# A two-layer streaming encoder trunk: full-height matmuls in attention, and another opening

## The chip, the cores and the metric

One core of a Trainium2 chip runs the whole program. The metric is the device time of one execution in microseconds (us); the kernel before is given by the median of three runs. The engines are named PE (matmul), PEld (loading of a matmul's stationary operand, which can overlap PE), DVE (vector), ACT (scalar), POOL (GpSimd) and SP (the queue from which nearly all transfers are issued).

## The reference, cut to what matters

544 tokens (512 of a prompt, 32 of a running stream, "the sample") go through two layers. What the change touches is the attention of each layer:

```python
q = einsum('blr,rc->blc', rmsnorm(cq, q_norm_l), w_uq_l)      # 8 heads, 128 + 64 wide
q_nope, q_pe = q[..., :128], rope(q[..., 128:], pos)
lat_new, kpe_new = rmsnorm(ckv, kv_norm_l), rope(kr, pos)     # 256 wide; 64 wide, shared by the heads
# prompt: 512 queries on 512 keys, chunks of 64 masked; sample: 32 queries on 128 cached + 32 new keys
s = (einsum('bqhd,bkhd->bhqk', q_nope, k_nope) + einsum('bqhr,bkr->bhqk', q_pe, k_pe)) * scale
o = einsum('bhqk,bkhd->bqhd', softmax(s), v)
```

Ahead of the first layer's combined input projection stands an RMSNorm, whose sum of squares over 1024 features is the other thing touched:

```python
h = x * rsqrt(mean(x * x, axis=-1) + EPS) * norm_mix_l
cq, ckv, kr, hq, hf, hi, hg, ga, gb = split(h @ w_in_l, ...)
```

## The kernel before, in words

Features lie on the 128 partitions and tokens along them. Each float32 operand of a large product is split into a high part (rounded to the matmul's format, a copy on ACT) and a low part (the rest, a subtraction on DVE, or on POOL for attention's weights), and a product is three matmuls: high by high, high by low, low by high. `linear` (L198) runs such products over 8 row blocks and two halves of 272 tokens; `load_w` fetches a weight tile and splits it (L175 on ACT, L176 on DVE or POOL). Weight tiles of one kind share three raw buffers and four buffers each for high and low parts.

**The opening.** The input comes in eight blocks x_0 to x_7, by SP, with a vector of small constants (`vec`) and the first weight tile (`raw_first`) between x_0 and x_1. For every block `prep` makes hhi (ACT, L263) and hlo (DVE, L264). Squares of the blocks (ACT L279 for the even ones, POOL or DVE L281 for the odd ones) are added on POOL and DVE (L283, L284), a matmul with ones (`pn_m`, L234) sums over partitions, and a square root and a reciprocal give the norm's factor r. Products hf, hq and hi of layer 0 run ahead of r; hg needs a PSUM bank that is freed only when hf has been multiplied by r.

**Attention.** Heads are taken one after another. `attend` is a generator whose ten steps are laid between the products of other work (merge gates, the second branch's projection, queries and keys of the next head). `block(qb)` makes the scores of 128 queries (L736 to L738), masks them, and calls `softmax` (DVE maximum, ACT exponential with sum, DVE reciprocal and multiplication, L719 to L723). The rotary part has the queries in one tile `q4` of four 32-row bands (high, high, low, low) and the keys in `krh` (128 rows: the 64 rows twice) and `krl` (64 rows):

```python
nc.tensor.matmul(ps, q4[:, qs], krh[:, ks], start=False, stop=False)
nc.tensor.matmul(ps, q4[0:64, qs], krl[:, ks], start=False, stop=True)
```

`turn` transposes the probabilities on PE (L764) and splits them, `weigh` multiplies them with the values (L778). The sample's 32 queries are the last rows of the last 128: `sample_scores` makes their scores for 160 keys with the same five matmuls, copies 32 rows out of PSUM and runs the softmax on them; `sample_turn` transposes 128 and 32 keys apart (L799, L800) and splits twice; `sample_weigh` (L812) runs three matmuls over 128 rows and three over 32. One score is thus five matmuls, of which the fifth has 64 rows; there are 4 blocks and one sample score for each of 8 heads and 2 layers, 80 in all.

The order on each engine is fixed when the kernel is built: a list scheduler places every instruction by its own estimate of when it can run, starting from the order of the code; on the chip each engine then takes its list strictly in order.

Of the kernel before, what the change touches and what calls it, by code (L numbers as in the profile page):

```python
# [9 lines left out]
F32 = mybir.dt.float32  # L10
F32R = mybir.dt.float32r
U8 = mybir.dt.uint8
AF = mybir.ActivationFunctionType
# [38 lines left out]
class Late:  # L52
    """A value whose instructions come with its first use, or within the product before."""
# [10 lines left out]
class Pieces:  # L64
    """Weights of n row blocks, of which each group of eight is fetched at its first use."""
# [13 lines left out]
class Side:  # L79
    """Work whose instructions are laid between those of the large products."""  # L80
# [8 lines left out]
    def pace(self, rate):  # L89
        """Steps to take for each tick of the large products."""  # L90
        self.rate, self.owed = rate, 0.0
# [23 lines left out]
def trunk(ctx, tc, io):  # L115
# [17 lines left out]
    one = tmp.tile([P, P], F32, tag="t", name="one")  # L133
    nc.vector.memset(one, 1.0)
    ones = const.tile([P, P], F32R, name="ones")
    nc.scalar.copy(ones, one)
    eps = const.tile([P, 1], F32, name="eps")
    nc.vector.memset(eps, EPS)

# [99 lines left out]
    class Norm:  # L239
        """Sum of squares over feature blocks, as they come."""  # L240
# [16 lines left out]
    def prep(x, gcol, norm, name, vector=False):  # L257
        """Split of gain * x, and its share of the norm's sum."""
# [7 lines left out]

    norm = Norm("in")
    h = []
    xs = [bt(f"x_{j}", F32) for j in range(ND)]
    nc.sync.dma_start(xs[0], io["x"][:, 0, :])  # L270
    nc.sync.dma_start(vec, io["vec"])
    first = fetch_w(io["w_in"][0, U_HF], ND * P, "first")
    for j in range(1, ND):
        nc.sync.dma_start(xs[j], io["x"][:, j, :])
    for j in range(ND):
        h.append(prep(xs[j], V_MIX + j, None, f"in{j}"))
    for j in range(ND):
        if j % 2 == 0:
            nc.scalar.activation(xs[j], xs[j], AF.Square)  # L279
        else:  # L280
            (nc.gpsimd if j < 4 else nc.vector).tensor_mul(xs[j], xs[j], xs[j])  # L281
    for j in range(2, ND):
        (nc.gpsimd if j < 6 else nc.vector).tensor_add(xs[j % 2], xs[j % 2], xs[j])  # L283
# [12 lines left out]
    # Lower bounds of the forget gates: softmax over the layers, cumulated.  # L296
# [34 lines left out]
    for l in range(L):  # L331
# [21 lines left out]
        if l == 0:  # L353
            # The first products run while the norm is still on its way.
            early[U_HF] = product(U_HF, "hf0_", first)
# [9 lines left out]
        with ExitStack() as mixer:  # L365
# [4 lines left out]
            krl = mp.tile([64, KW], F32R, name=f"krl{l}")  # L370
# [729 lines left out]
```

## Time and profile before

| | |
|---|---|
| median of three runs (lowest, highest) | 1913.16 us (1912.61, 1913.16) |
| span of the profiled execution | 1910.8 us |
| PE busy, PEld busy | 1887.2 us (99%), 1847.6 us (97%) |
| DVE, ACT, POOL busy | 1092.7 us (57%), 797.1 us (42%), 312.2 us (16%) |
| chain that ended last | PE 97%, DVE 1%, DMA 1% |
| mean granted TensorE clock | 0.997 |

Times are counted from the span's start. In rows of the timeline the columns are start, duration, engine, line, operation, written tile <- read tiles, size (rows*columns of the stationary operand where it is a matmul) and, in brackets, how long the engine had been idle and what ended that. Matmuls are pipelined, so their printed durations overlap: what one costs on PE is the distance from its start to the next one's. In rows of busy times by stretch stand the stretch, its length, the busy time of PE, PEld, DVE, ACT and POOL with the number of instructions, the granted TensorE clock as a share of full speed, the busy share of the DMA engines and their GB/s.

### The profile page before, as it was taken

To read this page: it belongs to the slowest core of one execution; us is meant where nothing else is said; L and a number is where in the kernel's file an instruction comes from. 1 tells how busy PE (TensorE), PEld (TensorE's weight loads), DVE (VectorE), ACT (ScalarE), POOL (GpSimd) and SP (SyncE) were. 2 spreads that over 40 slices of the span, in tenths; PEclk is the share of its full clock that TensorE was granted. 3 is DMA by queue.
4 is the path that set the end of the run, shared out by engine and by line. 5 is a ranking of instruction groups with operands and counts; after the bars stand their busy time and mean duration, and the time that the engine had idled before them with its cause. 6 is when DMAs were issued, how large, how long until landed. Compare 5 with 4: busy or idle time off the path is not lost.

```text
span 1910.8 us, 36056 instructions
## 1 busy us (share of the span) xinstructions
PE 1887.2 (99%) x14680; PEld 1847.6 (97%) x14680; DVE 1092.7 (57%) x2113; ACT 797.1 (42%) x1454; POOL 312.2 (16%) x474
## 2 busy tenths in 40 slices
PE   7999999999999999999999999999999999999997
PEld 7999999899999999999999999998999999999997
DVE  7765865666465555533375667656655655555224
ACT  4222866554344333332232248564533433333231
POOL 3011021221212222100011110212112122222001
PEclk9999999999999999999999999999999999999999
DMA  5121432333542222234322124323235422222332
GB/s 181 57 70 67 131 122 83 95 102 104 194 158 89 89 89 89 89 95 125 102 91 70 57 80 143 119 80 107 93 126 190 138 85 87 87 88 87 103 96 75
DMA packets 75526, 197.29 MB, mean 103 GB/s; under 512 B 10208, under 2 KB 14304, under 8 KB 75360
## 3 DMA queue, kind: packets, MB, share of 16 engines
q1 hardware_dynamic: 75360, 194.98, 30.9%
q8 instruction: 116, 1.90, 0.4%
q14 instruction: 50, 0.41, 0.1%
HBM read 165.68 MB, written 24.81 MB: 100 GB/s over the span
## 4 chain that ended last, share of the span: by engine, by line
PE 97%; DVE 1%; DMA 1%; issue 0%; SPq 0%; ACT 0%; DVEq 0%; ACTq 0%
PE ps_uv L198 14%; PE ps_ua L198 14%; PE ps_d L198 13%; PE ps_gate L198 10%; PE ps_pa L198 5%; PE ps_o L198 5%; PE A L401 3%; PE ps_q L198 3%; PE ps_pb L198 3%; PE ps_hg L198 3%; PE ps_hq L198 2%; PE ps_hi L198 2%; PE ps_hf L198 2%; PE ps_cq L198 2%; PE sc L736 2%; PE ps_v L710 2%
## 5 line engine op out<-in xcount | busy, mean ns | idle before, releaser
L176 DVE TENSOR_TENSOR wlo_d<-raw_d,whi_d 128x512 fp32r<-128x512 f32 x96 | 62.5, 655 | 149.5 <-ACT whi_d L175 149.5
L198 PE MATMUL ps_uv<-hlo_f,whi_uv 128*128 128x272 f32 x704 | 145.9, 289 | 0.0
L198 PE MATMUL ps_ua<-hlo_f,whi_ua 128*128 128x272 f32 x704 | 145.9, 289 | 0.0
L198 PE MATMUL ps_ua<-hhi_f,wlo_ua 128*128 128x272 f32 x704 | 145.8, 288 | 0.0
L198 PE MATMUL ps_ua<-hhi_f,whi_ua 128*128 128x272 f32 x704 | 145.6, 288 | 0.0
L198 PE MATMUL ps_uv<-hhi_f,whi_uv 128*128 128x272 f32 x704 | 145.6, 288 | 0.0
L198 PE MATMUL ps_uv<-hhi_f,wlo_uv 128*128 128x272 f32 x704 | 145.4, 288 | 0.0
L198 PE MATMUL ps_d<-il,whi_d 128*128 128x272 f32 x660 | 136.9, 289 | 0.0
L198 PE MATMUL ps_d<-ih,wlo_d 128*128 128x272 f32 x660 | 136.6, 288 | 0.0
L198 PE MATMUL ps_d<-ih,whi_d 128*128 128x272 f32 x660 | 136.2, 288 | 0.0
L175 ACT CAST whi_d<-raw_d 128x512 fp32r<-128x512 f32 x96 | 55.8, 585 | 175.5 <-PE ps_d L198 143.7
L175 ACT CAST whi_ua<-raw_ua 128x512 fp32r<-128x512 f32 x88 | 54.7, 621 | 165.3 <-PE ps_ua L198 157.9
L175 ACT CAST whi_uv<-raw_uv 128x512 fp32r<-128x512 f32 x96 | 59.6, 621 | 142.5 <-PE ps_uv L198 134.1
L198 PEld LDWEIGHTS ps_ua<-hhi_f,wlo_ua 128*128 128x128 f32 x704 | 110.8, 188 | 0.2
L198 PEld LDWEIGHTS ps_ua<-hhi_f,whi_ua 128*128 128x128 f32 x704 | 110.9, 188 | 0.0
L198 PEld LDWEIGHTS ps_uv<-hhi_f,whi_uv 128*128 128x128 f32 x704 | 110.9, 188 | 0.0
L198 PEld LDWEIGHTS ps_uv<-hhi_f,wlo_uv 128*128 128x128 f32 x704 | 110.7, 188 | 0.0
L198 PEld LDWEIGHTS ps_ua<-hlo_f,whi_ua 128*128 128x128 f32 x704 | 110.4, 188 | 0.0
L198 PEld LDWEIGHTS ps_uv<-hlo_f,whi_uv 128*128 128x128 f32 x704 | 110.4, 188 | 0.0
L198 PEld LDWEIGHTS ps_d<-ih,whi_d 128*128 128x128 f32 x660 | 103.6, 188 | 0.0
L198 PEld LDWEIGHTS ps_d<-il,whi_d 128*128 128x128 f32 x660 | 103.6, 188 | 0.0
L198 PEld LDWEIGHTS ps_d<-ih,wlo_d 128*128 128x128 f32 x660 | 103.2, 188 | 0.0
(469 smaller groups left out, 5274.8 us busy)
## 6 DMA issues: line engine op xcount, KB each, us to landing
raw_ua<-in_w_up SPq DMA_DIRECT2D x44, 512.0 KB, 3.2
raw_uv<-in_w_up SPq DMA_DIRECT2D x44, 512.0 KB, 3.2
raw_gate<-in_w_in SPq DMA_DIRECT2D x32, 512.0 KB, 3.7
raw_d<-in_w_dn SPq DMA_DIRECT2D x32, 512.0 KB, 3.5
gates<-z_gate SPq DMA_DIRECT2D x32, 272.0 KB, 2.9
raw_pa<-in_w_pa SPq DMA_DIRECT2D x16, 512.0 KB, 3.5
raw_wo<-in_w_o SPq DMA_DIRECT2D x16, 512.0 KB, 3.7
raw_d<-in_w_dn SPq DMA_DIRECT2D x16, 384.0 KB, 3.1
```

The source lines that it names most:

```text
L175: nc.scalar.copy(hi[:, :n], part)
L176: (nc.gpsimd if pool else nc.vector).tensor_sub(lo[:, :n], part, hi[:, :n])
L198: nc.tensor.matmul(ps[t][:, 0:n], w, x[:, t * n:(t + 1) * n], start=(i == 0), stop=(i == last),)
L401: nc.tensor.matmul(ps[:, s], kk[:, s], qq[:, s], start=True, stop=True)
L710: nc.tensor.matmul(ps[:, :2 * P], lat[k][x][:, s], wv[k][w], start=(i == 0), stop=(i == 5))
L736: nc.tensor.matmul(ps, a[:, qs], b[:, ks], start=(i == 0), stop=False)
```

## The change

In attention: `krl` gets 128 rows (the low part of both copies of the rotary keys), and the fifth matmul of a score reads all of `q4`. The sample's softmax runs on all 128 rows straight from PSUM, into a buffer of the probabilities' own pool of four (a 96-column strip of it is zeroed on POOL); its two transposes are 128 by 128, its split is one copy and one subtraction, and all six of its weighing matmuls read 128 rows. In the opening: `raw_first` comes in two halves, both issued from ACT's queue; its splits stand right behind the first block's hhi and hlo in the code; all squares are on ACT, all additions on DVE, none on POOL. Docstrings and comments are dropped too, so line numbers differ by a few.

```diff
+    first = wts.tile([P, 1024], F32, tag="raw", name="raw_first", bufs=3)
     nc.sync.dma_start(xs[0], io["x"][:, 0, :])
+    nc.scalar.dma_start(first[:, 0:512], io["w_in"][0, U_HF][:, 0:512])
     nc.sync.dma_start(vec, io["vec"])
-    first = fetch_w(io["w_in"][0, U_HF], ND * P, "first")
+    nc.scalar.dma_start(first[:, 512:1024], io["w_in"][0, U_HF][:, 512:1024])
...
     for j in range(ND):
         h.append(prep(xs[j], V_MIX + j, None, f"in{j}"))
+        if j == 0:
+            first_ws = load_w(None, ND, P, "hf0_0", raw=first)
     for j in range(ND):
-        if j % 2 == 0:
-            nc.scalar.activation(xs[j], xs[j], AF.Square)
-        else:
-            (nc.gpsimd if j < 4 else nc.vector).tensor_mul(xs[j], xs[j], xs[j])
-    for j in range(2, ND):
-        (nc.gpsimd if j < 6 else nc.vector).tensor_add(xs[j % 2], xs[j % 2], xs[j])
+        nc.scalar.activation(xs[j], xs[j], AF.Square)
+        if j > 1:
+            nc.vector.tensor_add(xs[j % 2], xs[j % 2], xs[j])
...
-            krl = mp.tile([64, KW], F32R, name=f"krl{l}")
+            krl = mp.tile([P, KW], F32R, name=f"krl{l}")
...
-                    nc.vector.tensor_sub(krl, kr[0:64, :], krh[0:64, :])
+                    nc.vector.tensor_sub(krl, kr, krh)
...
-                        nc.tensor.matmul(ps, q4[0:64, qs], krl[:, ks], start=False, stop=True)
+                        nc.tensor.matmul(ps, q4[:, qs], krl[:, ks], start=False, stop=True)
...
-                        sP = ap.tile([SS, NK], F32, tag="sP", name=f"sP{nm}")
-                        nc.scalar.copy(sP, ps[P - SS:P, :NK])
-                        softmax(sP, sP, SS, f"{nm}_s")
+                        sP = ap.tile([P, 512], F32, tag="p", name=f"sP{nm}", bufs=4)
+                        nc.gpsimd.memset(sP[:, NK:2 * P], 0.0)
+                        softmax(sP[:, :NK], ps[:, :NK], P, f"{nm}_s")
...
-                        nc.tensor.transpose(ps[:, 0:SS], sP[:, 0:PAST], ident[0:SS, 0:SS])
-                        nc.tensor.transpose(ps[0:SS, SS:2 * SS], sP[:, PAST:NK], ident[0:SS, 0:SS])
+                        for a in range(2):
+                            nc.tensor.transpose(pw[:, a, :], sP[:, a * P:(a + 1) * P], ident)
...
-                        split(sph[:, 0:SS], spl[:, 0:SS], ps[:, 0:SS])
-                        split(sph[0:SS, SS:2 * SS], spl[0:SS, SS:2 * SS], ps[0:SS, SS:2 * SS])
+                        split(sph, spl, pw[:, :, P - SS:P])
...
-                        for a, rr in ((0, P), (1, SS)):
+                        for a in range(2):
...
-                                    ps[:, 0:SS], v[0:rr, 4 + a, vo:vo + P], p[0:rr, a * SS:(a + 1) * SS],
+                                    ps[:, 0:SS], v[:, 4 + a, vo:vo + P], p[:, a, :],
```

Where instructions move, first ACT in the opening, before (`x` tiles are the input blocks; L279 is a square, L263 an hhi, L175 the split of a weight tile's half):

```order
L263 ACTIVATE hhi_in_116<-x_91,vec 128x544
L279 ACTIVATE x_89<-x_89 128x544
L263 ACTIVATE hhi_in_120<-x_92,vec 128x544
L279 ACTIVATE x_91<-x_91 128x544
L263 ACTIVATE hhi_in_124<-x_93,vec 128x544
L175 CAST whi_hq_0_0_237<-raw_hq_0_235 128x512
L263 ACTIVATE hhi_in_128<-x_94,vec 128x544
L279 ACTIVATE x_93<-x_93 128x544
L263 ACTIVATE hhi_in_132<-x_95,vec 128x544
L175 CAST whi_hq_0_4_241<-raw_hq_0_235 128x512
```

And the same engine after the change, from the fifth hhi on (L256 is an hhi, L284 a square, L168 a split):

```order
L256 ACTIVATE hhi_in_133<-x_87,vec 128x544
L284 ACTIVATE x_85<-x_85 128x544
L256 ACTIVATE hhi_in_137<-x_88,vec 128x544
L284 ACTIVATE x_86<-x_86 128x544
L256 ACTIVATE hhi_in_141<-x_89,vec 128x544
L284 ACTIVATE x_87<-x_87 128x544
L256 ACTIVATE hhi_in_145<-x_90,vec 128x544
L284 ACTIVATE x_88<-x_88 128x544
L284 ACTIVATE x_89<-x_89 128x544
L168 CAST whi_hq_0_0_238<-raw_hq_0_236 128x512
L284 ACTIVATE x_90<-x_90 128x544
L168 CAST whi_hq_0_4_242<-raw_hq_0_236 128x512
```

The split of the second product's weights (whi_hq) has moved from between the hhi's to behind all of them and behind seven of the eight squares.

PE at the end of product hf and the beginning of product hq, before:

```order
L198 MATMUL ps_hf_0_186<-hhi_in_128,wlo_hf_0_4_183 128x272 x2
L198 MATMUL ps_hq_0_245<-hhi_in_108,whi_hq_0_0_237 128x272
L198 MATMUL ps_hf_0_186<-hlo_in_129,whi_hf_0_4_182 128x272 x2
L198 MATMUL ps_hq_0_245<-hhi_in_108,whi_hq_0_0_237 128x272
L198 MATMUL ps_hf_0_186<-hhi_in_132,whi_hf_0_4_182 128x272 x2
L198 MATMUL ps_hf_0_186<-hhi_in_132,wlo_hf_0_4_183 128x272 x2
L198 MATMUL ps_hq_0_245<-hhi_in_108,wlo_hq_0_0_238 128x272 x2
L198 MATMUL ps_hq_0_245<-hlo_in_109,whi_hq_0_0_237 128x272 x2
```

And after:

```order
L191 MATMUL ps_hf_0_187<-hhi_in_145,whi_hf_0_4_117 128x272 x2
L191 MATMUL ps_hf_0_187<-hhi_in_145,wlo_hf_0_4_118 128x272 x2
L191 MATMUL ps_hf_0_187<-hlo_in_146,whi_hf_0_4_117 128x272 x2
L191 MATMUL ps_hq_0_246<-hhi_in_109,whi_hq_0_0_238 128x272 x2
L191 MATMUL ps_hq_0_246<-hhi_in_109,wlo_hq_0_0_239 128x272 x2
L191 MATMUL ps_hq_0_246<-hlo_in_110,whi_hq_0_0_238 128x272 x2
```

Before, matmuls of hq stand in the gaps of hf from the sixth block on; after, none of hq stands ahead of hf's last.

POOL in attention, layer 0, while head 2 is attended to (wlo tiles are low parts of weights: qr the rotary queries of heads 4 to 7, qk head 4's queries and keys), after the change:

```order
L169 TENSOR_TENSOR wlo_pb_1_0_4153<-raw_pb_1_4150,whi_pb_1_0_4152 128x512
L169 TENSOR_TENSOR wlo_qr_1_0_0_4232<-raw_qr_1_4229,whi_qr_1_0_0_4231 128x384
L796 MEMSET sP_2_4108 128x96
L169 TENSOR_TENSOR wlo_qr_1_1_0_4236<-raw_qr_1_4229,whi_qr_1_1_0_4235 128x384
L169 TENSOR_TENSOR wlo_qk_4_0_4384<-raw_qk_4_4381,whi_qk_4_0_4383 128x512
L169 TENSOR_TENSOR wlo_qk_4_4_4388<-raw_qk_4_4381,whi_qk_4_4_4387 128x128
```

The zeroing of the sample's strip is new on this engine and stands among the splits; the splits keep their order.

## Rows read from the trace of the kernel before

**Rows 1.** Busy us by stretch: PE, PEld, DVE, ACT, POOL, then clock; attention, feed-forward, attention.

```profile
281.00:469.00 188.00, 187.09 (x1311) 169.67 (x1310) 118.16 (x350) 99.78 (x264) 29.36 (x31) 1.00 0.31 96
560.00:824.00 264.00, 264.00 (x2095) 263.84 (x2094) 144.86 (x244) 102.08 (x156) 54.38 (x127) 1.00 0.26 90
1223.00:1411.00 188.00, 187.07 (x1313) 169.54 (x1312) 118.26 (x350) 99.72 (x264) 29.37 (x31) 1.00 0.30 96
```

**Rows 2.** Timeline of PE: end of one block's score and start of the next.

```profile
318.19 0.28 PE L736 MATMUL sc<-kl,qh 128*128 128x256 f32 x1
318.31 0.28 PE L737 MATMUL sc<-krh,qr 128*128 128x256 f32 x1
318.52 0.38 PE L738 MATMUL sc<-krl,qr 64*128 64x256 f32 x1
318.83 0.38 PE L736 MATMUL sc<-kh,qh 128*128 128x256 f32 x1
319.06 0.28 PE L736 MATMUL sc<-kh,ql 128*128 128x256 f32 x1
```

**Rows 3.** Timeline of PEld, the loads of two of these matmuls.

```profile
318.19 0.19 PEld L737 LDWEIGHTS sc<-krh,qr 128*128 128x128 f32 x1
318.52 0.18 PEld L738 LDWEIGHTS sc<-krl,qr 64*128 64x128 f32 x1
```

**Rows 4.** Instructions that read tile krl: blocks of the prompt.

```profile
L738 PE MATMUL sc<-krl,qr x64: 379/408/498, 294.0 to 1398.4; 64*128 64x256 f32 x32, 64*128 64x384 f32 x16, 64*128 64x512 f32 x16
```

**Rows 5.** Timeline of PE: three full transposes, later the sample's two (at 312.33).

```profile
310.39 0.49 PE L764 MATMUL pt<-ident,p 128*128 128x128 f32 x3
...
310.98 0.41 PE L198 MATMUL ps_gate<-hhi_in,wlo_gate 128*128 128x272 f32 x2
...
311.99 0.41 PE L198 MATMUL ps_gate<-hlo_in,whi_gate 128*128 128x272 f32 x2
...
312.89 0.41 PE L198 MATMUL ps_gate<-hhi_in,wlo_gate 128*128 128x272 f32 x2
```

**Rows 6.** Timeline of PE: first of the sample's six weighing matmuls, and what follows.

```profile
315.58 0.18 PE L812 MATMUL spo<-sph,vh 128*128 128x32 f32 x1
...
316.34 0.52 PE L198 MATMUL ps_q<-cqh,whi_qk 128*128 128x272 f32 x2
316.70 0.41 PE L198 MATMUL ps_q<-cqh,wlo_qk 128*128 128x272 f32 x2
```

**Rows 7.** Timeline of DVE: the last step of two softmaxes, head 2.

```profile
347.46 0.53 DVE L723 TENSOR_SCALAR p<-p,st 128x128 f32<-128x128 f32 x2
```

**Rows 8.** Timeline of PE: the first transpose of their result.

```profile
348.04 0.27 PE L764 MATMUL pt<-ident,p 128*128 128x128 f32 x1
```

**Rows 9.** Timeline of POOL: a weight split that waited for transposes.

```profile
422.35 0.46 POOL L176 TENSOR_TENSOR wlo_qk<-raw_qk,whi_qk 128x128 fp32r<-128x128 f32 x1 [4.91 <-PE pt L764]
```

**Rows 10.** Timeline of ACT in the opening.

```profile
4.32 0.30 ACT L309 ACTIVATE lb_e<-lb_e 128x4 f32<-128x4 f32 x2 [2.00 <-DVE lb_e L308]
6.33 1.14 ACT L175 CAST whi_hf<-raw_first 128x512 fp32r<-128x512 f32 x2 [1.71 <-DMA raw_first<-in_w_in]
7.37 2.02 ACT L263 ACTIVATE hhi_in<-x,vec 128x544 fp32r<-128x544 f32 x3
9.30 0.64 ACT L279 ACTIVATE x<-x 128x544 f32<-128x544 f32 x1
...
12.95 0.62 ACT L175 CAST whi_hq<-raw_hq 128x512 fp32r<-128x512 f32 x1 [1.17 <-DMA raw_hq<-in_w_in]
```

**Rows 11.** Timeline of DVE in the opening.

```profile
8.19 2.17 DVE L264 SCALAR_TENSOR_TENSOR hlo_in<-x,vec,hhi_in 128x544 fp32r<-128x544 f32 x3
...
15.12 1.85 DVE L264 SCALAR_TENSOR_TENSOR hlo_in<-x,vec,hhi_in 128x544 fp32r<-128x544 f32 x1
```

**Rows 12.** Timeline of PE: the matmuls with ones, behind products hf and hq.

```profile
26.95 1.08 PE L234 MATMUL pn_m<-x,ones 128*128 128x272 f32 x4
```

**Rows 13.** Busy times of a stretch within product hq (columns as in rows 1).

```profile
18.10:21.40 3.30, 3.07 (x14) 2.75 (x13) 3.30 (x4) 0.66 (x1) 1.84 (x2) 0.50 0.00 0
```

More of the change, by code (lines that the diff above doesn't have):

```diff
@@ L132, in trunk @@
     masks = const.tile([P, 8, P], U8, name="masks")
[L133 to L138, printed above, removed]
     def bt(name, dtype=F32R):
@@ L269, in trunk @@
     xs = [bt(f"x_{j}", F32) for j in range(ND)]
+    first = wts.tile([P, 1024], F32, tag="raw", name="raw_first", bufs=3)
     nc.sync.dma_start(xs[0], io["x"][:, 0, :])
+    nc.scalar.dma_start(first[:, 0:512], io["w_in"][0, U_HF][:, 0:512])
     nc.sync.dma_start(vec, io["vec"])
-    first = fetch_w(io["w_in"][0, U_HF], ND * P, "first")
+    nc.scalar.dma_start(first[:, 512:1024], io["w_in"][0, U_HF][:, 512:1024])
+    one = tmp.tile([P, P], F32, tag="t", name="one")
+    nc.vector.memset(one, 1.0)
+    ones = const.tile([P, P], F32R, name="ones")
+    nc.scalar.copy(ones, one)
+    eps = const.tile([P, 1], F32, name="eps")
+    nc.vector.memset(eps, EPS)
     for j in range(1, ND):
         nc.sync.dma_start(xs[j], io["x"][:, j, :])
+    first_ws = []
     for j in range(ND):
         h.append(prep(xs[j], V_MIX + j, None, f"in{j}"))
+        if j == 0:
+            first_ws = load_w(None, ND, P, "hf0_0", raw=first)
     for j in range(ND):
-        if j % 2 == 0:
-            nc.scalar.activation(xs[j], xs[j], AF.Square)
-        else:
-            (nc.gpsimd if j < 4 else nc.vector).tensor_mul(xs[j], xs[j], xs[j])
-    for j in range(2, ND):
-        (nc.gpsimd if j < 6 else nc.vector).tensor_add(xs[j % 2], xs[j % 2], xs[j])
+        nc.scalar.activation(xs[j], xs[j], AF.Square)
+        if j > 1:
+            nc.vector.tensor_add(xs[j % 2], xs[j % 2], xs[j])
     nc.vector.tensor_add(xs[0], xs[0], xs[1])
@@ L353, in trunk @@
         if l == 0:
-            early[U_HF] = product(U_HF, "hf0_", first)
+            early[U_HF] = linear(first_ws, h, TH, "ps_hf0_0")
             early[U_HQ] = product(U_HQ, "hq0_")
@@ L798, in sample_turn @@
                         ps = s_ps(f"spt{nm}")
-                        nc.tensor.transpose(ps[:, 0:SS], sP[:, 0:PAST], ident[0:SS, 0:SS])
-                        nc.tensor.transpose(ps[0:SS, SS:2 * SS], sP[:, PAST:NK], ident[0:SS, 0:SS])
-                        sph = ap.tile([P, 2 * SS], F32R, tag="sph", name=f"sph{nm}")
-                        spl = ap.tile([P, 2 * SS], F32R, tag="spl", name=f"spl{nm}")
-                        split(sph[:, 0:SS], spl[:, 0:SS], ps[:, 0:SS])
-                        split(sph[0:SS, SS:2 * SS], spl[0:SS, SS:2 * SS], ps[0:SS, SS:2 * SS])
+                        pw = ps[:, 0:2 * P].rearrange("p (a q) -> p a q", a=2)
+                        for a in range(2):
+                            nc.tensor.transpose(pw[:, a, :], sP[:, a * P:(a + 1) * P], ident)
+                        sph = ap.tile([P, 2, SS], F32R, tag="sph", name=f"sph{nm}")
+                        spl = ap.tile([P, 2, SS], F32R, tag="spl", name=f"spl{nm}")
+                        split(sph, spl, pw[:, :, P - SS:P])
                         return sph, spl
```

## The prediction

> **What bounds the kernel now.** I read the page's busy shares first, then busy times by stretch, then the timeline of PE where the stretches differ, then the opening. PE is busy nearly everywhere, so time is won only by making PE's stream shorter or by filling the few places where it waits. In the feed-forward part that stream is dense: 2095 matmuls in 264.00 us, 0.126 us each, and the weight loads (PEld) fill the same 264 us to within 0.16. In the two attention stretches PE is also called busy (187.09 and 187.07 of 188), but PEld has 18.33 and 18.46 us without a load [rows 1]. The reader is to see there 36.8 us in which a matmul unit that reads as full starts nothing. The timeline tells where: inside a score, matmuls of 256 columns start 0.12 apart, but the fifth, of 64 rows, starts 0.21 after the fourth, what follows it starts 0.31 later, and the next one another 0.23 later [rows 2].
>
> **The change part by part.**
>
> *Scores.* The surplus of one 64-row visit is (0.21 - 0.12) + (0.31 - 0.12) + (0.23 - 0.12) = 0.39 us. The matmul keeps its columns, and columns set the distance of its full-height neighbours, so with 128 rows I expect 0.12 where now 0.31 stands. There are 64 such matmuls in the prompt's blocks [rows 4] and 16 in the sample's scores: 80 x 0.39 = 31.2 us, all of it on PE, where nothing lies beside it. The wider `krl` subtraction works on more partitions at the same length and costs nothing that the end sees.
>
> What the loads do speaks for this. The load of the full-height fourth matmul starts at 318.19, 0.12 before its matmul and while the third is under way; the load of the 64-row one starts with its matmul, at 318.52 [rows 2, 3]. A load is hidden behind the matmul before it as long as the height stays the same, and exposed where it changes. The Trainium skill says the contrary (TensorE: Matmul & The Clock Gate, "Part 3: Packing small matmuls"): a weight load overlaps with matmuls in flight only when it goes to another group of rows. By that rule full-height loads behind full-height matmuls would be exposed too, and more rows would win nothing of the 31.2; the rows above show them hidden, so the sum goes by the rows.
>
> *The sample's transposes.* They stand between pairs of ordinary matmuls: from 311.99 to 312.89 are 0.90 us, less two pairs at 0.25 leaves 0.40 for two small transposes and the changes of height. Three full transposes, with one ordinary pair, take 310.39 to 310.98 = 0.59, less 0.25 = 0.34, so 0.11 each [rows 5]. Two full ones cost 0.23; saved 0.17 x 16 = 2.7 us.
>
> *The sample's weighing.* Six matmuls of 32 columns from 315.58 to 316.70, less the ordinary pair in it, take 0.87 [rows 6]; six at the transposes' 0.11 take 0.67; saved 0.20 x 16 = 3.2 us.
>
> Together 37.1 us. The other way to the same number is PEld's idle time, 36.8, of which up to 1.8 is PE really waiting (0.91 and 0.93) and stays: 35.0 at least. I take 36, with 35 to 37.1 as ends.
>
> *What comes late next.* The softmax chains don't get faster, and PE now reaches their results sooner. For head 2 the last DVE step ends at 347.46 + 0.53 = 347.99 and the first transpose starts at 348.04 [rows 7, 8]: 0.05 us of margin, where the scores ahead of it become shorter by one surplus or two. So part of the gain returns as waiting at the first transposes of a head; later ones stand further behind their softmax. The trace doesn't show such a wait. Its bounds: nothing, as DVE has 118 us of work in 188 [rows 1] and a shift once taken serves the rest of the head; or one surplus of 0.39 for each of 16 heads, 6.2. I take 3, the middle: the one margin read is thin, but a head has ten steps in which PE can be early or late. The sample's chain itself loses a copy on ACT and one of its two splits on ACT and on DVE; it keeps its PSUM bank until the exponential, as every block does. I cost that at nothing: cover is the step of attention that lies between.
>
> *The zeroing on POOL.* 16 small instructions on an engine that is busy for 29.4 of 188 us [rows 1]. Each waits for the transposes of the buffer's former tenant, and the weight splits of the next head are queued behind it. Those transposes stand earlier on PE than the matmuls that need the splits, so PE passes the point before it needs anything from POOL. Cost nothing; without that cover, the price of the third rival.
>
> *The opening.* Before, the matmuls with ones, behind hf and hq, start at 26.95 [rows 12]. What delays hf and hq is DVE: an hlo takes 2.17 / 3 = 0.72 alone and 1.85 beside POOL's additions [rows 11]. After, POOL is out of it and ACT's list sets the pace. Its terms: `raw_first` lands at 6.33, and ACT had been free for 1.71 us [rows 10], so an earlier issue on a queue of its own gains between 0 and 1.7; I take 0.8, half of it, so 5.5. (The Trainium skill, DMA: Bandwidth & Descriptors, "Issuing engines are not separate DMA queues", has it that another queue saves only the issue, as all share the same 16 engines. By that the gain would be nearer to the lower end.) Both halves are split before anything else, the second in 0.52 (1.14 for two overlapping casts), then two small exponentials, 0.3, so the first hhi starts at 6.3. From there ACT does eight hhi, eight squares and the split of the first half of raw_hq. Start to start an hhi takes 0.64 (three in 2.02, the last 0.73 long), a square 0.55 (9.30 to the next hhi), a split 0.52: 8 x 0.64 + 8 x 0.55 + 0.52 = 10.0, so 16.3. Then DVE adds the last square and makes raw_hq's low part, 0.7 each by rows 11, and may be one step behind: 18.0. Product hq needs that low part for its third matmul, and none of hq can stand in hf's gaps any more. The remaining 46 matmuls take 5.8 us at 0.126: 23.8. But PE has then half idled for 1.5 us, and before, after such idling, a stretch of 3.3 us shows the granted clock at 0.50, the lower level of 1.2 GHz, and only 14 matmuls [rows 13], where 26 would fit: 1.5 us lost. With it 25.4, a gain of 1.5 against 26.95; without it 3.1; with no earlier landing and one more step behind, 0. Everything behind the matmuls with ones keeps its distances: the square root, the reciprocal, hg's wait for its bank. I take 1.5, from 0 to 3.1.
>
> *Sum.* 36 - 3 + 1.5 = 34.5 us from the profiled execution's 1910.8 gives 1876.3. The median lies 2.4 above that execution's span; with it 1878.7.
>
> **The rivals.**
>
> 1. *Attention becomes bound by the softmax chain.* DVE and ACT hold as much work in 18 us less per layer. For it: the 0.05 us of margin, and a DVE share that rises from 118 of 188 to 118 of 170. Against: 30% of DVE would still be free, and PE waited for under 1 us per stretch. If half of the 36 returns as waiting: 1913.2 - 18 - 1.5 = 1893.7.
>
> 2. *Height is not what costs.* The surplus would belong to the end of a score, such as its last matmul into a bank, and full-height loads would not hide; this is the skill's rule of above at work. Then only the opening gains: 1913.2 - 1.5 = 1911.7, within 0.2%. Against it: the same surplus stands around the sample's transposes and in its weighing where the height goes from 128 to 32 [rows 5, 6], which are not ends of scores.
>
> 3. *Slower: the zeroing holds back the next head's weights.* A split on POOL waited 4.91 us for transposes once [rows 9]. If each of 16 zeroings holds the splits behind it as long, and PE is left waiting for all of that, it adds 16 x 4.9 = 78 us: 1913.2 - 37.5 + 78 = 1954. It decides from 37.5 / 16 = 2.3 us per head on. Against: POOL is idle most of the time, and the transposes come first on PE.
>
> **How the numbers follow.** The forecast, 0.86: 1878.7. Its own ends are 1913.2 - 37.1 - 3.1 = 1873.0 and 1913.2 - 35 + 6.2 = 1884.4. Rival 1 0.07, rival 2 0.04, rival 3 0.03. The range goes a little further on both sides for durations that differ from one execution to another and for the near part of rival 1: 1872 to 1887. 0.2% of the time, 3.8 us, is about what a measurement of this kernel can tell from no change. Faster: forecast and rival 1, 0.93; same: rival 2, 0.04; slower: rival 3, 0.03.
>
> **What would show each step.** Scores: five matmuls of a block 0.12 apart, the load of the fifth ahead of its matmul, PEld busy for nearly all of attention. Sample: two transposes 0.11 apart, six weighing matmuls 0.11 apart. Waits: idle time of PE ahead of the first transposes, ended by DVE, 3 us in all. Opening: hlo's of under 0.8 throughout, PE waiting once, about 1.5 us, at hq's low part, and the matmuls with ones at about 25.4. The prediction is wrong if the fifth matmul still starts 0.21 after the fourth, if PE waits for tens of microseconds on probabilities, or if splits on POOL come late behind the zeroing.

## The result

| | before | after |
|---|---|---|
| median of the runs compared (lowest, highest) | 1912.88 us (1912.3, 1913.16), 4 runs | 1878.85 us (1878.01, 1879.76), 4 runs |
| ratio, with its 95% interval | | 0.9823 (0.9809 to 0.9837) |
| span of the profiled execution | 1910.8 us | 1876.2 us |

The time fell by 34.0 us; 34.5 were forecast (1878.7). Of all executions in this document one is left out, that of the sample alone which was profiled: it took 3049.8 us at a mean granted clock of 0.557, so no row of that kernel is shown. The page's first lines after the change:

```profile
span 1876.2 us, 36067 instructions
PE 1852.0 (99%) x14680; PEld 1840.5 (98%) x14680; DVE 1089.1 (58%) x2099; ACT 789.9 (42%) x1426; POOL 304.8 (16%) x484
```

PE's busy time fell by 35.2 us, from 1887.2, and PEld's by only 7.1, from 1847.6: most of what went is time in which PE read as busy and no load ran. The same by stretch, with the columns of [rows 1] (attention, feed-forward, attention):

```profile
278.00:454.00 176.00, 173.88 (x1341) 170.16 (x1340) 119.98 (x345) 96.50 (x251) 33.14 (x41) 1.00 0.33 103
535.00:799.00 264.00, 264.00 (x2102) 263.84 (x2101) 145.62 (x242) 102.75 (x157) 54.41 (x125) 1.00 0.28 92
1204.00:1379.00 175.00, 172.84 (x1333) 169.03 (x1332) 119.37 (x343) 96.16 (x250) 32.30 (x41) 1.00 0.33 103
```

In attention PEld is now without a load for 5.84 and 5.97 us, where it had been 18.33 and 18.46. The feed-forward stretch is as full as it was, with one small difference: 2102 matmuls start in its 264 us instead of 2095, so they are 0.1256 us apart instead of 0.1260. In PE's timeline the places that answer to [rows 5, 6] and [rows 2] read as follows (the sample's two transposes ahead of an ordinary product; the first of its six weighing matmuls and what follows them; the end of a score and the start of the next):

```profile
308.08 0.38 PE L804 MATMUL spt<-ident,sP 128*128 128x128 f32 x2
308.22 0.50 PE L191 MATMUL ps_gate<-hhi_in,whi_gate 128*128 128x272 f32 x2
308.55 0.41 PE L191 MATMUL ps_gate<-hhi_in,wlo_gate 128*128 128x272 f32 x2
...
311.24 0.18 PE L815 MATMUL spo<-sph,vh 128*128 128x32 f32 x1
...
311.83 0.50 PE L191 MATMUL ps_q<-cqh,whi_qk 128*128 128x272 f32 x2
312.16 0.41 PE L191 MATMUL ps_q<-cqh,wlo_qk 128*128 128x272 f32 x2
...
313.41 0.28 PE L739 MATMUL sc<-kh,qh 128*128 128x256 f32 x1
...
313.76 0.28 PE L740 MATMUL sc<-krh,qr 128*128 128x256 f32 x1
313.88 0.28 PE L741 MATMUL sc<-krl,qr 128*128 128x256 f32 x1
314.00 0.28 PE L739 MATMUL sc<-kh,qh 128*128 128x256 f32 x1
314.12 0.28 PE L739 MATMUL sc<-kh,ql 128*128 128x256 f32 x1
```

The two transposes and the pair behind take 308.55 - 308.08 = 0.47, less 0.25 for the pair 0.22, where 0.40 stood; the six weighing matmuls 312.16 - 311.24 - 0.25 = 0.67, where 0.87 stood. Starts within these scores, of 256 columns, are all 0.12 apart, where 0.21, 0.31 and 0.23 stood. And PEld's row of the fifth load, which answers to [rows 3]:

```profile
313.77 0.19 PEld L741 LDWEIGHTS sc<-krl,qr 128*128 128x128 f32 x1
```

It starts at 313.77, 0.11 ahead of its matmul: hidden.

What PE waits for, by the view of waits (waiting tile, what it waited for, then us in total, times, longest), two rows of the kernel before, then five rows of after, four of them of the same kinds:

```profile
PE pt L764 <- DVE ptl L154: 1.4, 2, 0.7
PE ps_pb L198 <- DVE kl L154: 0.5, 2, 0.2
```

```profile
PE pt L767 <- DVE p L726: 2.5, 4, 0.9
PE ps_hq L191 <- DVE wlo_hq L169: 1.4, 1, 1.4
PE pt L767 <- DVE ptl L147: 0.7, 2, 0.3
PE ps_pb L191 <- DVE ql L147: 0.6, 2, 0.3
PE ps_pb L191 <- DVE kl L147: 0.4, 2, 0.2
```

The first row is the wait that was forecast: a head's transposes (`pt`) wait for the last step of the softmax (`p`), four times. The second is the opening's. The opening of after, by engine (ACT, DVE, PE; columns as in [rows 10 to 12]):

```profile
4.84 0.62 ACT L168 CAST whi_hf<-raw_first 128x512 fp32r<-128x512 f32 x1 [1.58 <-DMA raw_first<-in_w_in]
5.74 0.62 ACT L168 CAST whi_hf<-raw_first 128x512 fp32r<-128x512 f32 x1 [0.29 <-DMA raw_first<-in_w_in]
6.47 2.01 ACT L256 ACTIVATE hhi_in<-x,vec 128x544 fp32r<-128x544 f32 x3
```

```profile
8.14 2.94 DVE L257 SCALAR_TENSOR_TENSOR hlo_in<-x,vec,hhi_in 128x544 fp32r<-128x544 f32 x4
16.18 1.98 DVE L286 TENSOR_TENSOR x<-x,x 128x544 f32<-128x544 f32 x3
18.09 0.68 DVE L169 TENSOR_TENSOR wlo_hq<-raw_hq,whi_hq 128x512 fp32r<-128x512 f32 x1
```

```profile
7.25 0.82 PE L191 MATMUL ps_hf<-hhi_in,whi_hf 128*128 128x272 f32 x2 [7.25 <-ACT hhi_in L256]
18.82 0.52 PE L191 MATMUL ps_hq<-hhi_in,wlo_hq 128*128 128x272 f32 x2 [1.45 <-DVE wlo_hq L169]
24.72 1.08 PE L227 MATMUL pn_m<-x,ones 128*128 128x272 f32 x4
```

An hlo takes 2.94 / 4 = 0.74, PE waits once for hq's low part, and the matmuls with ones start at 24.72, 2.23 ahead of [rows 12].

### The profile page after: what moved, and what is told of

Read it like the earlier page. It is cut to its first block, busy times and chain, and to the rows that moved or that the text cites. A ratio compares the mean times of both kernels' runs of the same rounds, so it can differ in the third digit from the quotient of the medians.

```text
span 1876.2 us, 36067 instructions
## 1 busy us (share of the span) xinstructions
PE 1852.0 (99%) x14680; PEld 1840.5 (98%) x14680; DVE 1089.1 (58%) x2099; ACT 789.9 (42%) x1426; POOL 304.8 (16%) x484
## 4 chain that ended last, share of the span: by engine, by line
PE 96%; DVE 3%; issue 1%; ACT 0%; DMA 0%; DVEq 0%; ACTq 0%
PE ps_ua L191 14%; PE ps_uv L191 14%; PE ps_d L191 13%; PE ps_gate L191 10%; PE ps_pa L191 5%; PE ps_o L191 5%; PE A L404 3%; PE ps_hg L191 3%; PE ps_pb L191 3%; PE ps_hq L191 3%; PE ps_hf L191 2%; PE ps_hi L191 2%; PE ps_q L191 2%; PE ps_cq L191 2%; PE ps_v L713 2%; PE po L781 2%
## 5 line engine op out<-in xcount | busy, mean ns | idle before, releaser
L168 ACT CAST whi_d<-raw_d 128x512 fp32r<-128x512 f32 x96 | 55.8, 585 | 175.6 <-PE ps_d L191 144.1
L168 ACT CAST whi_ua<-raw_ua 128x512 fp32r<-128x512 f32 x88 | 54.7, 622 | 164.8 <-PE ps_ua L191 157.4
L168 ACT CAST whi_uv<-raw_uv 128x512 fp32r<-128x512 f32 x96 | 59.7, 622 | 142.0 <-PE ps_uv L191 133.6
```

Of the source, the lines that this page charges most:

```text
L168: nc.scalar.copy(hi[:, :n], part)
```

## The experiments

The kernel before ran beside all of them, with medians of 1912.75 to 1912.87 us in the four batches; 1912.8 is used below.

| kernel | median us | ratio to before (95%) |
|---|---|---|
| scores alone | 1887.7 | 0.9870 (0.9857 to 0.9884) |
| sample alone | 1906.7 | 0.9968 (0.9956 to 0.9981) |
| opening alone | 1910.7 | 0.9987 (0.9978 to 0.9996) |
| attention without opening | 1882.1 | 0.9840 (0.9827 to 0.9854) |
| two matmuls of 64 rows per score | 1912.9 | 0.9999 (0.9990 to 1.0008) |
| zeroing eightfold | 1880.0 | 0.9825 (0.9808 to 0.9841) |
| opening: off POOL only | 1910.3 | 0.9986 (0.9978 to 0.9995) |
| opening: halves only | 1912.7 | 0.9999 (0.9990 to 1.0008) |
| after, hq's weights first | 1876.6 | 0.9809 (0.9794 to 0.9824) |
| the same, first tile in one piece | 1877.4 | 0.9814 (0.9801 to 0.9828) |
| hq's weights first, 24 matmuls ahead | 1876.1 | 0.9807 (0.9792 to 0.9822) |
| the same, fourth block early | 1878.2 | 0.9819 (0.9806 to 0.9833) |

### The scores alone

```diff
-            krl = mp.tile([64, KW], F32R, name=f"krl{l}")
+            krl = mp.tile([P, KW], F32R, name=f"krl{l}")
...
-                    nc.vector.tensor_sub(krl, kr[0:64, :], krh[0:64, :])
+                    nc.vector.tensor_sub(krl, kr, krh)
...
-                        nc.tensor.matmul(ps, q4[0:64, qs], krl[:, ks], start=False, stop=True)
+                        nc.tensor.matmul(ps, q4[:, qs], krl[:, ks], start=False, stop=True)
```

> The kernel before with one part of the change alone: krl gets 128 rows and the fifth matmul of every score reads all of q4. The theory (each change of height of the stationary operand exposes weight loads, 0.386 us per visit of a block score and 0.356 of a sample score in the trace of before): 64 x 0.386 + 16 x 0.356 = 30.4 us less, of which 2 to 3 us return as waits of PE for probabilities; so 1912.9 - 28 = 1885, between 1882 and 1888. If height is not what costs (the surplus belongs to the end of a score): 1912.9, no change. If attention were bound by the softmax chain: half of it, 1898.

1887.7 us, 25.1 less: height is what costs. That is within the range given, but 2.9 short of the 28 expected. Start to start, taken against the usual spacing of matmuls of the same width, the surplus of all scores falls as foreseen (64 block scores from 0.39 each to nothing, 16 sample scores from 0.356 to 0.04, together 29.9 us), so 4.8 us come back. Part of it is a new row among the waits:

```profile
PE pt L764 <- DVE p L723: 1.8, 4, 0.6
```

### The sample alone

```diff
-                        sP = ap.tile([SS, NK], F32, tag="sP", name=f"sP{nm}")
-                        nc.scalar.copy(sP, ps[P - SS:P, :NK])
-                        softmax(sP, sP, SS, f"{nm}_s")
+                        sP = ap.tile([P, 512], F32, tag="p", name=f"sP{nm}", bufs=4)
+                        nc.gpsimd.memset(sP[:, NK:2 * P], 0.0)
+                        softmax(sP[:, :NK], ps[:, :NK], P, f"{nm}_s")
...
-                        for a, rr in ((0, P), (1, SS)):
+                        for a in range(2):
```

> The kernel before with the sample's edits alone: softmax of all 128 rows straight from PSUM, the zeroed strip, two 128 by 128 transposes, one split, six weighing matmuls of 128 rows. The 64-row matmul of the scores stays. The theory: 16 x (0.178 + 0.20) = 6.0 us less, with little of it back as waits: 1907, between 1906 and 1908.5. If height is not what costs: larger transposes cost more and nothing is won, 1913 or a little more. If the zeroing on POOL held back the next head's weights: slower than 1913.

1906.7 us, 6.1 less, as large as the two terms (2.85 for transposes and 3.2 for weighing, by the starts in the traces of before and after). Nothing of it comes back: the new softmax, the zeroing and the wait for a buffer of the common pool are all covered.

### The opening alone, and attention without it

The first has the opening's hunks of the diff and nothing else, the second all the others.

> The kernel before with the opening's edits alone: first weight tile in two halves issued from ACT's queue and split behind the first block, all squares on ACT, all additions on DVE. The theory: the matmuls with ones move from 26.95 to about 24.7 us and everything behind them keeps its distances, so 1912.9 - 2.2 = 1910.7. If the opening's gain is taken back later in layer 0 (products that are ahead there wait elsewhere): 1912.9. If the gain seen in the opening of the changed kernel was partly owed to attention's edits (none is known): less than 1.

> The changed kernel with the opening of the kernel before; all of attention's edits stay. The theory: the parts add up, so 1878.9 + 2.2 = 1881.1, between 1880 and 1882. If the scores' part and the sample's part share the same waits, the sum of the parts (runs of each alone) is larger than this run's gain by up to 3 us; if they don't touch each other, the two gains add up to 31.8 within 1 us.

1910.7 and 1882.1. The gains are 2.0 and 30.7 us, and the scores and the sample by themselves give 25.1 + 6.1 = 31.2. These times alone don't settle whether the parts add up, since the four executions of attention without the opening lie at 1880.9, 1881.1, 1883.1 and 1883.7. The traces do. From the start of the first score to the start of the last weighing matmul of a layer, both layers together, the kernel before takes 347.1 us (292.84 to 466.45, 1235.03 to 1408.50), the scores alone 25.2 less, attention without the opening 31.3 less and the changed kernel 31.3 less (290.59 to 448.50, 1215.96 to 1373.84). So the sample adds 6.1 there, as much as by itself: the parts share no gain and no wait, and the opening changes next to nothing in attention.

Together 30.7 + 2.0 = 32.7, against 34.0 for the whole; the 1.3 between are within the spread of these runs, and the opening differs from one execution to the next. In the profiled execution of the opening alone the matmuls with ones stand at 26.59, not at 24.72, and this stretch is in it (columns as in [rows 1]):

```profile
20.50:24.50 4.00, 4.00 (x22) 4.00 (x21) 1.33 (x3) 0.62 (x1) 0.00 (x0) 0.58 0.75 217
```

The granted clock is 0.58 on average, near its lower level of 1.2 GHz, a little more than 1 us behind PE's wait for hq's low part (it starts again at 19.19 there), and pairs of matmuls are 0.45 apart in it instead of 0.25. That is the loss that I forecast for the opening, and at its price: from the end of that wait to the matmuls with ones it is 26.59 - 19.19 = 7.40 there and 24.72 - 18.82 = 5.90 in the changed kernel, 1.5 more. (The other 0.4 of the distance to 24.72 was there before the stretch.) The changed kernel's profiled execution simply doesn't have it. The runs of the opening alone fall into groups that fit this: five of eleven from 1909.4 to 1909.9, five from 1910.7 to 1911.1 (the profiled one is of these), one at 1912.3. The four runs of the changed kernel are 1878.0 (the profiled one), 1878.3, 1879.4 and 1879.8.

Before, what the same loss costs depends on where it falls, as three executions of the same opening show. Attention without the opening has no low stretch where [rows 13] have 0.50, and starts its matmuls with ones at 26.83, only 0.12 ahead of [rows 12]:

```profile
18.10:21.40 3.30, 2.09 (x15) 1.65 (x13) 3.30 (x4) 0.66 (x1) 1.76 (x1) 1.00 0.00 0
```

There PE works for 2.09 of 3.30 us and waits for DVE; a slower PE fills its waits first. In the profiled execution of the scores alone the low stretch comes later and reaches into the dense part of hq:

```profile
19.80:25.30 5.50, 5.50 (x23) 5.37 (x24) 5.50 (x8) 1.25 (x2) 1.13 (x1) 0.50 0.37 113
```

Its matmuls with ones start at 28.73, 1.78 behind [rows 12]. Of that, 0.27 was there when the stretch began (PE goes on at 19.79 behind its wait for an hlo, and at 19.52 in the trace of before), so the stretch costs 1.5 more there than before. This execution is the slowest of the four, 1889.3 against 1887.4 to 1887.8.

### Two matmuls of 64 rows

```diff
-                        nc.tensor.matmul(ps, q4[:, qs], krh[:, ks], start=False, stop=False)
+                        nc.tensor.matmul(ps, q4[0:64, qs], krh[0:64, ks], start=False, stop=False)
```

> The kernel before with both rotary matmuls of a score on 64 rows (the fourth too: the queries' high rows by the keys' high rows; the product of the queries' low part with the keys' high part is left out). Two 64-row matmuls now stand side by side between 128-row ones. If the price belongs to the change of height (once down, once up per score): the surplus per score stays near 0.39 and the time near 1912.8, at most 1 or 2 us off. If it belongs to every 64-row load: twice the surplus, 30 us more, 1943. If it belonged to the end of a score: 1912.8 as well, but then the run with full-height scores would not have won its 25 us.

1912.9 us, no change. The timeline of PE, one score and the start of the next:

```profile
317.68 0.28 PE L736 MATMUL sc<-kh,qh 128*128 128x256 f32 x1
...
318.14 0.38 PE L737 MATMUL sc<-krh,qr 64*128 64x256 f32 x1
318.36 0.28 PE L738 MATMUL sc<-krl,qr 64*128 64x256 f32 x1
318.56 0.39 PE L736 MATMUL sc<-kh,qh 128*128 128x256 f32 x1
318.79 0.28 PE L736 MATMUL sc<-kh,ql 128*128 128x256 f32 x1
```

A score with one 64-row matmul takes 0.87 from first start to first start, or 318.83 in [rows 2] less 317.96 in the trace of before:

```profile
317.96 0.28 PE L736 MATMUL sc<-kh,qh 128*128 128x256 f32 x1
```

With two it takes 318.56 - 317.68 = 0.88. Their loads, and that of the matmul behind them, from PEld's timeline:

```profile
318.13 0.18 PEld L737 LDWEIGHTS sc<-krh,qr 64*128 64x128 f32 x1
318.24 0.19 PEld L738 LDWEIGHTS sc<-krl,qr 64*128 64x128 f32 x1
318.56 0.19 PEld L736 LDWEIGHTS sc<-kh,qh 128*128 128x128 f32 x1
```

The second 64-row load starts 0.12 ahead of its matmul, while the first one's matmul is under way; the loads at both changes of height start with their matmuls. The next start behind such a matmul comes 0.22 and 0.23 later, where 0.12 is usual. The price is thus not one of low matmuls. It is paid for going down and coming up again, once per visit, whether the visit has one low matmul or two.

### The zeroing eightfold

```diff
+                        for _ in range(8):
-                        nc.gpsimd.memset(sP[:, NK:2 * P], 0.0)
+                            nc.gpsimd.memset(sP[:, NK:2 * P], 0.0)
```

> The changed kernel with the zeroing of the sample's strip issued eight times instead of once, 112 more instructions on POOL. If its cover holds as I costed it (POOL idle for most of attention, the transposes that it waits for come first on PE): no change, 1878.9 within 1.5 us. If the splits of the next head's weights are held back: PE waits at the first product of a head, and the time rises by up to 112 times the zeroing's duration.

1880.0, 1.1 above the changed kernel. POOL has now 24 us of it, in the view of groups (busy us, mean ns; then the idle time ahead and what ended it):

```profile
L797 POOL MEMSET sP<- 128x96 f32 x128 | 24.0, 187 | 52.3 <-PE pt L767 46.0
```

112 more at 0.187 would be 21 us if they were in PE's way. PE's waits of attention are the same rows with the same 2.5 and 0.7 us as above, and from first score to last weighing both layers together take 0.3 us more. The profiled execution has its matmuls with ones at 26.70 instead of 24.72, with a granted clock of 0.66 from 20.5 to 24.5: nearly all of the 1.1 belongs to the opening. The third rival is out, and the cover holds for seven more of these instructions per head, 1.3 us.

### The two halves of the opening

First the squares and additions alone:

```diff
-        if j % 2 == 0:
-            nc.scalar.activation(xs[j], xs[j], AF.Square)
-        else:
-            (nc.gpsimd if j < 4 else nc.vector).tensor_mul(xs[j], xs[j], xs[j])
-    for j in range(2, ND):
-        (nc.gpsimd if j < 6 else nc.vector).tensor_add(xs[j % 2], xs[j % 2], xs[j])
+        nc.scalar.activation(xs[j], xs[j], AF.Square)
+        if j > 1:
+            nc.vector.tensor_add(xs[j % 2], xs[j % 2], xs[j])
```

> The kernel before with half of the opening's edits: squares on ACT, additions on DVE, none of them on POOL; the first weight tile still comes in one piece by SP. It asks what brought the opening's 2 us. If POOL's company is what slowed DVE (hlo 1.85 beside POOL's additions, 0.72 alone): hlo's of under 0.8 throughout, the matmuls with ones about 1 to 1.3 us earlier than 26.95, 1911.5 to 1912. If the earlier start of PE (8.17 to 7.25) is all: no change, 1912.8, or slower, as ACT has four squares more.

Then the halves on ACT's queue, with their splits behind the first block, alone:

```diff
...
+    nc.scalar.dma_start(first[:, 0:512], io["w_in"][0, U_HF][:, 0:512])
...
-    first = fetch_w(io["w_in"][0, U_HF], ND * P, "first")
+    nc.scalar.dma_start(first[:, 512:1024], io["w_in"][0, U_HF][:, 512:1024])
```

> The kernel before with the other half: the first weight tile in two halves on ACT's queue, split behind the first block; squares and additions stay on POOL and DVE as before. PE starts 0.9 us earlier. If DVE sets the pace beside POOL: PE waits for the same hlo's, which come at most 0.5 earlier, and the time stays within 0.5 us of 1912.8. If the start is what counts: 0.9 us less, 1911.9.

1910.3 and 1912.7. The first is all of the opening's gain, 2.5 us and more than the 0.8 to 1.3 expected; the second is worth nothing. In the first one's profiled execution, which has no low stretch, the matmuls with ones start at 25.08, 1.87 ahead of [rows 12]. Another 1.1 us are won where nothing was changed: from the last weighing of the first layer to the first score of the second it takes 767.5 us, and 768.6 before. The feed-forward part of the first layer has most of it: 264 us of it hold 2102 matmuls in this kernel, in the changed one and in that of the opening alone, which all have nothing on POOL in the opening, and 2095 before, with the scores alone, with attention without the opening and with the halves only, which have POOL in it. Why the spacing depends on an edit so far ahead of it is open. A row of each half, DVE's hlo in the first and, in the second, the step that waits for `vec` and the hlo's behind it:

```profile
8.22 2.17 DVE L264 SCALAR_TENSOR_TENSOR hlo_in<-x,vec,hhi_in 128x544 fp32r<-128x544 f32 x3
```

```profile
5.95 0.16 DVE L310 TENSOR_TENSOR lb_mx<-vec 128x4 f32<-128x4 f32 x1 [4.94 <-DMA vec<-in_vec]
...
8.65 5.51 DVE L258 SCALAR_TENSOR_TENSOR hlo_in<-x,vec,hhi_in 128x544 fp32r<-128x544 f32 x5
```

Without POOL an hlo takes 0.72 to 0.79 throughout. With the halves but beside POOL five take 5.51, 1.10 each, and they begin at 8.65, behind 8.19 in [rows 11]: PE starts at 7.33 instead of 8.17, and then waits 0.89 for the first hlo. The cause is a chain of a dozen small steps for the gates' lower bounds, which needs `vec`. Before, that came by 3.93 and the chain was done ahead of the weights' splits; with a second queue filled at the same time it comes by 5.95, and the chain stands in front of the first hlo. In the other traces too `vec` comes by 3.93 to 4.01 where the tile is in one piece, and by 5.33 to 5.95 where it is in halves.

Two rules of the Trainium skill bear on this. DMA: Bandwidth & Descriptors, section "Issuing engines are not separate DMA queues", says that transfers from all issuers share the same engines and that another issuer saves only the issuing. The trace agrees: in the changed kernel the second half was issued 0.47 us earlier than the whole tile had been (1.18 against 1.65) and came 0.59 earlier (5.74 against 6.33), and `vec` paid for it. SBUF — State Buffer, section "SBUF: two separate sides", says that a vector instruction with two inputs from this memory and a GpSimd instruction that reads it block each other for a whole instruction. The trace agrees in kind: 0.72 alone, 1.85 in [rows 11] beside an addition on POOL.

### Versions of the opening

hq's weights loaded and split ahead of the squares, on the changed kernel:

```diff
+    hq_ws = load_w(io["w_in"][0, U_HQ], ND, P, "hq0_0")
     for j in range(ND):
         nc.scalar.activation(xs[j], xs[j], AF.Square)
...
-            early[U_HQ] = product(U_HQ, "hq0_")
+            early[U_HQ] = linear(hq_ws, h, TH, "ps_hq0_0")
```

> The changed kernel with the loading and splitting of hq's weights written ahead of the squares instead of behind them, so that their low part no longer stands behind the last additions on DVE and products hf and hq can be interleaved. The theory: in the changed kernel PE waits 1.45 us there (18.82) because of that DVE step, so at least 1.45 us are won, up to 2.3 (48 pairs of matmuls from 7.25 on, 15 of them at the lower clock until 14.1, the rest at 0.25 each, end at 22.4 instead of 24.7): 1876.5 to 1877.5. The rival: the additions, now later, hold the matmuls with ones back, or hhi's late on ACT do, and nothing is won: 1879.

1876.6 us, 2.3 less than the changed kernel, and with a narrow spread (1876.2 to 1876.7). In the profiled execution there is no wait for hq's low part, and the granted clock stays at 1.00. The matmuls with ones:

```profile
23.09 1.08 PE L227 MATMUL pn_m<-x,ones 128*128 128x272 f32 x4
```

The same with the first tile in one piece by SP, as before the change:

> The version with hq's weights first (1876.6), with the first weight tile again in one piece by SP. The halves alone won nothing on the kernel before (1912.7), where DVE beside POOL set the pace; here POOL is out. The theory: they are worth nothing here too, since the first hlo on DVE starts at about the same time either way (8.22 with the tile in one piece and POOL out, 8.34 with the halves): 1876.6, within 0.5. The rival: with PE dense from its start on, the 0.9 to 1.1 us of later start (8.2 instead of 7.0) are paid in full: 1877.6.

1877.4: my theory was wrong here, and the rival nearer. Where DVE is no longer late, the halves are worth something, 0.8 us. How much of it the earlier start brings isn't settled: in the profiled execution, the slowest of five, PE starts 2.06 us later (9.08 against 7.02), but the matmuls with ones only 0.46 later (23.55), since pairs of hf are 0.45 apart until 12.87 there and until 14.30 in the other.

And with 24 matmuls ahead of the first product:

```diff
+    idle = s_ps("warm")
+    for i in range(24):
+        nc.tensor.matmul(idle[:, 0:P], ones, ones, start=(i == 0), stop=(i == 23))
```

> The same, and 24 matmuls of the ones tile by itself, into a bank that nobody reads, on PE ahead of the first product (work that the result doesn't need). They ask whether the granted clock in the opening is what sets PE's pace there: in the changed kernel the pairs of hf start 0.45 apart until 14.1 and 0.25 apart from then on. The theory: with the clock up at 7.3 PE follows ACT's list (an hhi and a square in 1.19), hf and hq end between 20.5 and 22: 1 to 2 us less than without them, 1875 to 1876.5. The rival: PE waits for ACT and DVE instead, the clock falls again in the gaps, and the time stays within 0.5 us of the run without them.

```profile
3.31 5.38 PE L275 MATMUL warm<-ones 128*128 128x128 f32 x24 [3.31 <-ACT ones L272]
22.11 1.08 PE L227 MATMUL pn_m<-x,ones 128*128 128x272 f32 x4
```

1876.1 us, 0.5 less again, at the edge of what these runs can tell apart (1875.7 to 1876.5 against 1876.2 to 1876.7), so they don't decide between the theory and its rival. Pairs of hf start 0.25 apart from 10.86 on, not only from 14.3 on as without them, but the extra matmuls hold the first product back to 8.50. It is the fastest kernel of this study.

### Where attention's gain was lost again

On top of that, the fourth block's scores ahead of the first transposes:

```diff
-                    turn(0, p01, (0,))
-                    yield
                     p23.append(block(3))
                     yield
+                    turn(0, p01, (0,))
+                    yield
```

> The version with hq's weights first and the 24 matmuls ahead, and in attention the scores of the fourth block ahead of the first transposes instead of behind them. It asks where the 5 us that attention's edits lost again went: in the changed kernel PE waits for probabilities in the heads in which little other work lies between the steps (0.5, 1.06 and 0.5 us, first transposes of both halves of the prompt). The theory: the fourth block's softmax has then one step more of time, its two waits of 0.9 go, 1 to 2 us less, 1874 to 1875. The rival: DVE is given a third softmax in a row, the first half's transposes wait for as long instead, no change (1876) or slower.

1878.2, 2.1 more, and the theory was wrong. The loss is in attention, where both layers take 317.1 us from first score to last weighing, against 315.0 without this edit. The rows of `pt` waiting for `p` are gone as expected, and these have come, the weighing waiting for the split of the transposed probabilities and the next head's values for theirs:

```profile
PE po L785 <- ACT pth L146: 1.5, 4, 0.4
PE ps_v L717 <- DVE vl L147: 1.5, 4, 0.5
```

So moving this one step doesn't remove the waits: the room given to one link of a head's chain (scores, softmax, transposes, split, weighing) was taken from the next. Other orders were not tried.

## Why the prediction was right, and where not

**What bounds the kernel.** Right: the 36.8 us in which PE read as busy and started nothing were for the most part the changes of height. The Trainium skill's rule (TensorE: Matmul & The Clock Gate, "Part 3: Packing small matmuls") that a load overlaps matmuls in flight only in another group of rows doesn't hold here: the fifth load, on the same 128 rows as the matmuls around it, starts 0.11 early. (The same section also has loads pulled ahead into a background weight buffer, which fits this row.) What a change of height needs was seen more closely with two 64-row matmuls side by side: one price per visit. The second way to the number, by PEld's idle time, agreed with the first partly by luck. PEld still has 11.8 us without a load, and PE's own idle time is only 4.3 of them, so some 7.5 us without a load are neither waiting nor a change of height.

**Scores.** 31.2 forecast, 29.9 measured. The block's surplus was right, the sample's scores had 0.356 and keep 0.04 at their narrower 160 columns.

**Sample.** 2.7 and 3.2 forecast; 2.85 and 3.2 by the traces, 6.1 by the run of that part alone.

**Waits.** 3 forecast, from 0 to 6.2. Between the first score and the last weighing matmul a layer took 173.6 and 173.5 us before and takes 157.9 twice now, 31.3 less in all; the terms above give 29.9 + 6.05 = 36.0, so 4.7 came back, and by the run with scores alone all of it belongs to the scores. The mechanism is as written (transposes that wait for the softmax's last step on DVE, from 0.05 us of margin on). The term was too small: I took the middle of my bounds for want of a row. The rows of waits shown above, 1.9 us before and 4.2 after in attention, account for half of it. Counted from start to start, the gaps of over 0.3 us at these places are 2.5 before and 5.9 after, 3.4 of the 4.7; where the rest lies is not shown.

**Zeroing, sample's chain.** Costed at nothing; nothing is what eightfold zeroing and the sample alone show.

**Opening.** 1.5 forecast; 2.2 at the matmuls with ones in the profiled execution, 2.0 by the median of the opening alone. The sum was near by luck, as its steps were not. The 0.8 for the earlier landing came about (5.74 for 5.5) and is worth nothing beside a late DVE, because `vec` came later. DVE was 0.8 later at hq's low part (18.77 for 18.0). And I charged 1.5 us for the lower clock as if it always came: the price was right, but the stretch comes in some executions and not in others, and the profiled one has none. Without it the sum as written would have been 23.8, and 24.72 was measured. Nor does ACT's list alone set the pace. Until 14.1 PE itself does, with pairs of matmuls 0.45 apart. Last, "everything behind the matmuls with ones keeps its distances" was wrong by the 1.1 us that the first layer's feed-forward gained.

**The sum** is right partly because errors cancel: 36 - 3 + 1.5 was forecast, and 36.0 - 4.7 + 2.2 + 1.1 = 34.6 is what the profiled executions' terms give, which is what the span fell by.

**The rivals.** Half of the gain lost to the softmax chain: no, 4.7 of 36. Height not the cost: no, by the scores alone. The zeroing on POOL: no, by eight of them.

## What to carry to other kernels

Look where an engine reads as busy and its companion (here the loads) doesn't: that gap can be won without less work, and a matmul that is made as high as its neighbours, with rows that add nothing wrong, costs no more than the low one. A gain on the busiest engine is partly handed back at the next link of the chain; cost it by the margin of that link, and don't expect to cure it by moving one step. Test the parts of an edit apart: of the two in the opening one brought everything and the other nothing, until a third made it worth 0.8 us. And read the clock of the very execution that is compared: the same loss cost 0.1 us here or 1.5, by what PE had to do beside it.

## What was not expected of the hardware

The price of another height does not grow with the number of low matmuls: 0.87 us for a score with one, 0.88 with two, 0.59 with none. A wait of 1.5 to 2 us on PE was followed in some executions by a stretch at the lower clock of 3 to 5.5 us, and in others with the same opening by none (1.86 in the trace of before with one, 1.98 in that of the two 64-row matmuls without). And from the program's start pairs of matmuls are 0.45 apart, as at the lower level, while the profile's column for the granted clock says 1.00: until 11.06 in the trace of before, until 14.14 in that of after. How long it lasts doesn't follow from when PE starts (8.17 and 7.25), and what decides it stays open. In the runs of the opening's edits, the dense matmuls of one stretch, some 500 us behind the only edit, started 0.1256 us apart instead of 0.1260; that is open too.
